# Four pairs of gate tiles as seven block products, and buffers of their own in all pairs of that form

## The chip, the cores and the metric

The kernel runs on one core of a Trainium2 chip. Such a core has TensorE (matrix products into eight accumulator banks), VectorE, ScalarE, GpSimd and SyncE, which work side by side, each through its own queue of instructions in order; transfers from memory run beside them on DMA queues that SyncE and GpSimd fill. In the profile the engines are PE (and PEld for its weight loads), DVE (VectorE), ACT (ScalarE), POOL (GpSimd) and SP (SyncE). The metric is the device time of one execution in microseconds.

## The reference

One decoder layer on x of 512 tokens by 1024 features, all in float32:

```python
proj = h @ w_in[l]
q, k, v, p, g = jnp.split(proj, [...], axis=-1)      # 512, 512, 512, 512 and 2 x 1024 columns
y_attn = moba_attention(q, k, v, rel_bias) @ w_branch_attn[l]
y_pool = multiscale_pool(p, w_pool_group[l], pool_scale[l]) @ w_branch_pool[l]
gates = sigmoid(g).reshape(B, S, 2, D)
mixed = gates[:, :, 0] * y_attn + gates[:, :, 1] * y_pool
h = layer_norm(ALPHA * h + mixed @ w_out[l], ln1_g[l], ln1_b[l])
a, u = jnp.split(h @ w_ffn_in[l], 2, axis=-1)        # 2 x 2816 columns
a = causal_dwconv(a, conv_w[l], conv_b[l])           # three taps along the tokens
f = (gelu(a) * u) @ w_ffn_out[l]
h = layer_norm(ALPHA * h + f, ln2_g[l], ln2_b[l])
```

The change concerns two products: the gate columns of `h @ w_in`, and `h @ w_ffn_in`.

## The kernel before

**Exact products from short ones.** TensorE multiplies operands of a shorter format (fp32r). So each float32 operand is split in two: ScalarE copies it to the short format (the high part, L69), VectorE subtracts that copy from the source (the low part, L70). A product is then three: high by high, high by low, low by high (`mm3`, L182 to 186). In the profile, rows of L184, L185 and L186 are these three.

**Weights.** All weights come in pieces of 128 by 1024, 512 KB, listed in `chunks` in the order of their use. `weights(i)` sees to it that the list has been fetched to LEAD = 3 pieces ahead; `fetch` takes the next: a load by SyncE into one of three raw buffers (`wraw`, L116), and the split into rings of five (`whi`, `wlo`). `state["limit"]` holds the fetching back where buffers further on do not exist yet.

**The stages.** x arrives transposed, is split, and stays as xT_hi and xT_lo. An input tile (`in_tile`) is 128 columns of w_in: 24 matmuls of 512 columns into a bank. `order` is the sequence of such tiles: q, k, p (pool) and 16 gate tiles, where the gate of feature block f has two tiles, f (attention branch) and 8 + f (pool branch). Attention works on four pairs of heads; `bg()` puts one input tile between its steps (scores, transposes of the weights P, product with V), so that TensorE has work while softmax runs. Behind the last product with V, which ends near 163 us, the remaining nine gate tiles run. The first twelve gate tiles are copied to `gates` by VectorE and their sigmoid is taken later; the last four (NLATE) go through ScalarE's sigmoid straight into `late`. zT (pool output) and oT (attention output) are split right behind attention. Then follow the branch products (br, with VectorE multiplying by the gates and GpSimd merging), the output projection (wo), layer norm, the feed-forward input, its output, and the last layer norm.

**Seven products in place of eight.** A feature block f of the feed-forward input is a pair: a and u, each 128 columns. With the tokens cut in halves (t1, t2) and the inner dimension cut in halves (k1, k2), the pair is a block product of 2 by 2, which can be formed with seven products of blocks in place of eight, when sums and differences of blocks are at hand. The pairs f = 4 to 17 (SEVEN) run in that form; the others are plain (48 matmuls of 512 columns). A pair in the form has four weight pieces:

- A, the chunk of a, loaded;
- X, a sum over halves of u and a: SyncE loads u's right half twice and GpSimd starts a second transfer that adds a's halves into it (`fetch_sums`, L129 to 133), into two buffers `xraw`; the two are issued AHEAD = 5 pieces early;
- D, the right half of u, loaded;
- Y, two sums by VectorE from X and A (L144), into a raw buffer.

Each is then split as any weight. The sums of the activations, T3, T4 and the negatives of T1 and T2 (`t_form`, L663 to 672), are formed and split once. `seven` (L688 to 718) issues 84 matmuls of 256 columns into three banks (sa, sb, sc in the profile), with ScalarE and VectorE adding partial results between them. The last product of a pair, `close`, waits in `pending` until the next pair has issued its second product.

**The order on each engine.** The program is not issued in the order of the Python text: a scheduler plays the program against a timeline of its own and puts each engine's instructions in the order in which they become ready there. Marks in the code can pin an instruction to the program's order or set one behind another. The order so built is fixed; on the chip, each queue works it off and waits where it must.

Of the kernel before, what the change touches and what calls it, by code (L numbers as in the profile page):

```python
# [14 lines left out]
P = 128  # L15
S = 512
# [29 lines left out]
def layer_kernel(ctx: ExitStack, tc: tile.TileContext, xT, x, w_v, w_c, rel_bias, invcnt, w_group,  # L46
# [18 lines left out]
    def split(hi, lo, src, copy=None):  # L65
        if copy:
            copy(hi, src)
        else:
            nc.scalar.activation(hi, src, AF.Copy)  # L69
        nc.vector.tensor_tensor(lo, src, hi.bitcast(F32), op=ALU.subtract)  # L70
# [6 lines left out]
    order += spare  # L77
# [4 lines left out]
    chunks += [w_c[first[n] + j] for n, j in order]  # L82
# [5 lines left out]
    fi_at = {}  # L88
    for f in range(NF):
        for q in "AXDY" if f in SEVEN else "au":  # L90
            fi_at[f, q] = len(chunks)
            chunks.append((f, q) if f in SEVEN else w_fi[2 * f + "au".index(q)])
# [30 lines left out]
    sums = list(SEVEN)  # L123
    xu = None

    def fetch_sums(f):
        x_ = raws[f, "X"] = xu.tile([P, D], F32, tag="xraw", name=f"xraw{f}", bufs=2)
        a, u = w_fi[2 * f], w_fi[2 * f + 1]
# [6 lines left out]
    def fetch_seven(i, f, q):  # L135
        n = S if q == "D" else D
        if q == "X":
            raw = raws[f, "X"]
        else:
            raw = raws[f, q] = wp.tile([P, D], F32, tag="wraw", name=f"wraw{i}", bufs=3)[:, :n]  # L140
        if q == "Y":
            a, x_ = raws[f, "A"], raws[f, "X"]
            for c, o in ((slice(0, S), x_[:, S:]), (slice(S, D), raw[:, :S])):
                nc.vector.tensor_tensor(raw[:, c], o, a[:, c], op=ALU.add)  # L144
        elif q != "X":
            nc.sync.dma_start(raw, w_fi[2 * f] if q == "A" else w_fi[2 * f + 1][:, S:])
# [3 lines left out]
        return hi, lo  # L150

# [30 lines left out]
    def mm3(out_, w, a, start, stop, **kw):  # L182
        (wh, wl), (ah, al) = w, a
        nc.tensor.matmul(out_, wh, ah, start=start, stop=False, **kw)  # L184
# [156 lines left out]
    def in_tile(n):  # L341
        kind, j = order[n]
        wh, wl = split3(weights(C0 + n), KT)
        b = bank(f"{kind}{j}")
        for kt in range(KT):
            mm3(b, (wh[:, kt, :], wl[:, kt, :]), (xT_hi[:, kt, :], xT_lo[:, kt, :]), kt == 0, kt == KT - 1)
# [6 lines left out]
        elif len(gslot) < NKEEP:  # L353
            gslot[j] = gates[:, len(gslot), :]
            nc.vector.tensor_copy(gslot[j], b)
# [55 lines left out]
    def pv(p):  # L411
# [7 lines left out]
        nc.scalar.activation(oT[:, p, :], b, AF.Copy)  # L419
# [5 lines left out]
    def bg(n=1):  # L425
        for _ in range(n):
            if len(todo) > NLATE:
# [6 lines left out]

    bg(3)
    for p in range(pairs):
# [7 lines left out]
        bg()  # L444
        pv(p)
    bg(len(todo))
# [486 lines left out]
```

## Time and profile before

| | |
|---|---|
| time, median of 3 runs | 650.57 us (650.09 to 651.02) |
| the profiled execution | 649.74 us, span 648.0 us |
| granted TensorE clock, mean | 0.996 |
| busy: PE, PEld, DVE, ACT, POOL | 98%, 85%, 69%, 51%, 17% |
| memory traffic over the span | 145 GB/s |

By stage, with TensorE's and VectorE's busy time:

| stretch (us) | what runs | PE busy | DVE busy |
|---|---|---|---|
| 0 to 163 | v, q, k, pool, seven gate tiles, attention | 160.9 | 95.5 |
| 163 to 212 | nine gate tiles; zT and oT split | 49.0 | 18.1 |
| 212 to 256 | branch products and merge | 44.0 | 28.5 |
| 256 to 347 | output projection, layer norm, plain feed-forward pairs | 91.0 | 66.6 |
| 347 to 488 | feed-forward pairs as seven products | 139.0 | 116.9 |
| 488 to 648 | last plain pairs, feed-forward output, layer norm | 151.8 | 123.9 |

The profile gives for each engine the time in which it was busy, and for each idle stretch the event that ended it. An idle time counts only where TensorE, or whatever ends last, stands still for it. In a list of waits, a row "PE sa L184 <- ACT whi L69: 1.9, 2, 1.1" reads: matmuls of line 184 into a bank of that name waited for ScalarE's copies of line 69, 1.9 us in all, twice, 1.1 us the longest. In a timeline, a row is the start in us, the duration, engine, line, operation, output and inputs with their shapes; in square brackets the idle time before it and what ended it. In a list of tiles, three numbers with strokes are the least, the median and the largest duration in ns. In a list of transfers, the last number is the median in us from issue to landing.

### The profile page before, as it was taken

How to read it: one execution, taken by the hardware profiler on the slowest of the kernel's cores; microseconds unless marked ns; L12 is line 12 of the kernel's file. 1: busy time of each engine (PE TensorE's matmuls, PEld its weight loads, DVE VectorE, ACT ScalarE, POOL GpSimd, SP SyncE). 2: the span in 40 equal slices, each digit the busy share in tenths (PEclk: the TensorE clock that was granted, in tenths of full speed). 3: DMA queues.
4: the chain of work that ended last, by engine and by line, in shares of the span. 5: the costliest groups of instructions: out<-in, count | busy, mean ns of one | idle time of the engine just before them, and what ended most of it. 6: DMA issues, size and time to landing. Idle time of an engine off the chain costs nothing.

```text
span 648.0 us, 9322 instructions
## 1 busy us (share of the span) xinstructions
PE 635.7 (98%) x3586; PEld 551.4 (85%) x3586; DVE 449.5 (69%) x666; ACT 328.0 (51%) x475; POOL 111.6 (17%) x153
## 2 busy tenths in 40 slices
PE   9999999999999999999999999999999999999994
PEld 6888787877888888888999999998998888888884
DVE  6466665564532576299667888787986859698596
ACT  6547556675522333215444556455665337465452
POOL 1605361211000123300010101010100201123302
PEclk9999999999999999999999999999999999999998
DMA  9643222212222227404056686677635895989905
GB/s 323 197 166 99 82 81 82 74 67 89 74 95 98 91 98 286 136 1 162 2 150 173 170 208 155 179 179 188 165 128 163 274 264 137 218 188 193 282 4 129
DMA packets 32540, 94.79 MB, mean 146 GB/s; under 512 B 3688, under 2 KB 3944, under 8 KB 32240
## 3 DMA queue, kind: packets, MB, share of 16 engines
q1 hardware_dynamic: 22832, 66.91, 30.4%
q0 software_dynamic: 9088, 26.24, 20.7%
q10 hardware_dynamic: 576, 1.05, 0.5%
q8 instruction: 28, 0.46, 0.3%
q14 instruction: 16, 0.13, 0.1%
HBM read 91.02 MB, written 3.17 MB: 145 GB/s over the span
## 4 chain that ended last, share of the span: by engine, by line
PE 91%; DVE 3%; POOL 2%; DMA 1%; ACT 1%; issue 1%; DVEq 0%; ACTq 0%; POOLq 0%
PE fi L186 5%; PE fi L184 5%; PE fi L185 5%; PE g L184 5%; PE g L186 4%; PE g L185 4%; PE sa L184 4%; PE sa L186 4%; PE sa L185 4%; PE v L285 3%; PE wo L186 2%; PE br L186 2%; PE br L184 2%; PE wo L184 2%; PE wo L185 2%; PE br L185 2%
## 5 line engine op out<-in xcount | busy, mean ns | idle before, releaser
L70 DVE TENSOR_TENSOR wlo<-wraw,whi 128x1024 fp32r<-128x1024 f32 (+1 forms) x119 | 144.1, 1214 | 59.2 <-ACT whi L69 57.7
L69 ACT ACTIVATE whi<-wraw 128x1024 fp32r<-128x1024 f32 (+1 forms) x118 | 117.2, 996 | 131.9 <-PE g L185 23.6
L186 PE MATMUL fi<-hT_hi,wlo 128*128 128x512 f32 (+1 forms) x168 | 56.7, 339 | 0.0
L185 PE MATMUL fi<-hT_lo,whi 128*128 128x512 f32 (+1 forms) x168 | 56.7, 339 | 0.0
L184 PE MATMUL fi<-hT_hi,whi 128*128 128x512 f32 (+1 forms) x168 | 56.4, 340 | 0.0
L184 PE MATMUL g<-xT_hi,whi 128*128 128x512 f32 x128 | 50.3, 393 | 0.0
L186 PE MATMUL g<-xT_hi,wlo 128*128 128x512 f32 x128 | 49.9, 390 | 0.0
L185 PE MATMUL g<-xT_lo,whi 128*128 128x512 f32 x128 | 49.8, 389 | 0.0
L132 POOL DMA_DIRECT2D xraw<-in_w_fi x14 | 17.0, 1215 | 183.7 <-DVE y L624 70.2
L69 ACT ACTIVATE whi<-tw 128x1024 fp32r<-128x1024 f32 (+1 forms) x30 | 29.4, 982 | 21.6 <-DMA tw<-in_w_fo 8.1
L70 DVE TENSOR_TENSOR wlo<-tw,whi 128x1024 fp32r<-128x1024 f32 (+1 forms) x30 | 33.3, 1127 | 8.4 <-ACT whi L69 8.4
L185 PEld LDWEIGHTS fi<-hT_lo,whi 128*128 128x128 f32 x168 | 31.9, 190 | 3.5
L186 PEld LDWEIGHTS fi<-hT_hi,wlo 128*128 128x128 f32 x168 | 31.9, 190 | 3.3
L184 PEld LDWEIGHTS fi<-hT_hi,whi 128*128 128x128 f32 x168 | 31.6, 190 | 3.3
L184 PE MATMUL sa<-hT_hi,whi 128*128 128x256 f32 x112 | 31.9, 285 | 2.0 <-ACT whi L69 1.9
L186 PE MATMUL sa<-hT_hi,wlo 128*128 128x256 f32 x112 | 31.7, 284 | 0.0
L185 PE MATMUL sa<-hT_lo,whi 128*128 128x256 f32 x112 | 31.6, 283 | 0.0
L184 PE MATMUL sb<-T_hi,whi 128*128 128x256 f32 x112 | 31.5, 282 | 0.0
L184 PE MATMUL sa<-nT_hi,whi 128*128 128x256 f32 x112 | 31.5, 281 | 0.0
L186 PE MATMUL sa<-nT_hi,wlo 128*128 128x256 f32 x112 | 31.3, 279 | 0.0
L185 PE MATMUL sa<-nT_lo,whi 128*128 128x256 f32 x112 | 31.3, 279 | 0.0
L185 PE MATMUL sb<-T_lo,whi 128*128 128x256 f32 x112 | 31.3, 279 | 0.0
(250 smaller groups left out, 1762.8 us busy)
## 6 DMA issues: line engine op xcount, KB each, us to landing
wraw<-in_w_fi SPq DMA_DIRECT2D x30, 512.0 KB, 3.6
wraw<-in_w_c SPq DMA_DIRECT2D x28, 512.0 KB, 3.4
tw<-in_w_fo POOLq DMA_DIRECT2D x20, 512.0 KB, 8.3
xraw<-in_w_fi SPq DMA_DIRECT2D x14, 512.0 KB, 4.9
xraw<-in_w_fi POOLq DMA_DIRECT2D x14, 512.0 KB, 5.7
wraw<-in_w_fo SPq DMA_DIRECT2D x10, 512.0 KB, 5.1
tw<-in_w_fo SPq DMA_DIRECT2D x10, 512.0 KB, 6.6
wraw<-in_w_br SPq DMA_DIRECT2D x8, 512.0 KB, 3.3
```

What stands on the lines that cost most here:

```text
L69: nc.scalar.activation(hi, src, AF.Copy)
L70: nc.vector.tensor_tensor(lo, src, hi.bitcast(F32), op=ALU.subtract)
L132: nc.gpsimd.dma_start(v, bass.AP(tensor=a.tensor, offset=a.offset, ap=[[pst, pn], [u.offset + S - a.offset, 2], [est, S]]), accum_op=ALU.add)
L184: nc.tensor.matmul(out_, wh, ah, start=start, stop=False, **kw)
L185: nc.tensor.matmul(out_, wh, al, start=False, stop=False, **kw)
L186: nc.tensor.matmul(out_, wl, ah, start=False, stop=stop, **kw)
L285: nc.tensor.matmul(bs[j], xs_[j][a], (wh, wl)[b], start=kt == 0 and n == 0, stop=False)
```

## The change

The gate pairs of features 4 to 7 (eight tiles, g4 to g7 and g12 to g15) run in the form of seven products, with x in place of the layer-normed activations. `order` now ends with g2, g10, g3, the four pairs ("s", 4) to ("s", 7), and g11. For this:

- The sums of x are formed behind attention: a pool `gx` takes attention's space, SyncE reloads xT in four quarters, `t_form` forms and splits the four sums; attention's last copy to oT is set behind the split of T3, and all later gate work with it. The X of pair 4 is fetched there too; `state["limit"]` holds back pair 4's weights while attention runs. One gate tile fewer runs ahead of the last product with V.
- `fetch_seven`, `s_mm`, `seven`, `t_form`, `pending` serve both stages; a pair is named by its stage and number.
- In both stages D has raw buffers of its own (two for the gates, one for the feed-forward), so that the three `wraw` hold A, Y and plain pieces; the first partial result has a tile p1 of its own in place of a part of y.
- The first matmul of D, and the first of a plain tile that stands while a `close` is pending, are pinned to the program's order. The split of nT1 comes last of the four.
- The zT and oT splits come behind the gates. A gate pair's sum goes through ScalarE's sigmoid as it is, u with a scale of -1, so no copy by VectorE and no later sigmoid is needed for the eight tiles; `late` is allocated earlier, on the other side of memory.

```diff
     spare = [("p", 2), ("p", 3)] + [("g", 8 * g + f) for f in range(KT) for g in range(2)]
     for p in range(1, pairs):
         order += [("q", p), ("k", p), spare.pop(0), spare.pop(0)]
-    order += spare
+    order += [("g", 2), ("g", 10), ("g", 3)] + [("s", f) for f in range(4, KT)] + [("g", 11)]
...
     chunks = [w_v[c] for c in range(4)]
     C0 = len(chunks)
-    chunks += [w_c[first[n] + j] for n, j in order]
+    at = {}
+    pair_of = {}
+    for n, j in order:
+        at[n, j] = len(chunks)
+        if n == "s":
+            pair_of["g", j] = w_c[first["g"] + j], w_c[first["g"] + KT + j]
+            for q in "AXDY":
+                at["g", j, q] = len(chunks)
+                chunks.append((("g", j), q))
+        else:
+            chunks.append(w_c[first[n] + j])
...
     def fetch(pool=None, early=None):
         i = state["next"]
         state["next"] = i + 1
-        while sums and xu and fi_at[sums[0], "X"] <= i + AHEAD:
+        while sums and sums[0][0] in xpool and at[(*sums[0], "X")] <= i + AHEAD:
             fetch_sums(sums.pop(0))
...
+    def fetch_sums(key):
+        x_ = raws[key, "X"] = xpool[key[0]](key[1])
+        a, u = pair_of[key]
...
-    def fetch_seven(i, f, q):
+    def fetch_seven(i, key, q):
         n = S if q == "D" else D
         if q == "X":
-            raw = raws[f, "X"]
-        else:
-            raw = raws[f, q] = wp.tile([P, D], F32, tag="wraw", name=f"wraw{i}", bufs=3)[:, :n]
+            raw = raws[key, "X"]
+        elif q == "D":
+            raw = dpool[key[0]](key[1])
+        else:
+            raw = raws[key, q] = wp.tile([P, D], F32, tag="wraw", name=f"wraw{i}", bufs=3)
         if q == "Y":
-            a, x_ = raws[f, "A"], raws[f, "X"]
+            a, x_ = raws[key, "A"], raws[key, "X"]
             for c, o in ((slice(0, S), x_[:, S:]), (slice(S, D), raw[:, :S])):
                 nc.vector.tensor_tensor(raw[:, c], o, a[:, c], op=ALU.add)
         elif q != "X":
-            nc.sync.dma_start(raw, w_fi[2 * f] if q == "A" else w_fi[2 * f + 1][:, S:])
+            a, u = pair_of[key]
+            nc.sync.dma_start(raw, a if q == "A" else u[:, S:])
         hi = wp.tile([P, D], F32R, tag="whi", name=f"whi{i}", bufs=RING)[:, :n]
         lo = wp.tile([P, D], F32R, tag="wlo", name=f"wlo{i}", bufs=RING)[:, :n]
         split(hi, lo, raw)
         return hi, lo
...
+    def t_form(n, tt, b11, b12, b21, b22):
+        if n in ("nT1", "T3"):
+            v, a = {"nT1": (b11, b11), "T3": (b12, b22)}[n]
+            nc.vector.tensor_tensor(v, a, b12, op=ALU.subtract)
+        else:
+            v, a = {"nT2": (b22, b11), "T4": (b21, b22)}[n]
+            nc.vector.scalar_tensor_tensor(v, a, -1.0, v, op0=ALU.mult, op1=ALU.subtract)
+        if n != "nT1":
+            split_of[n] = split(*tt[n], v)
+        if n == "T4":
+            split(*tt["nT1"], b11)
+
+    def s_mm(key, q, part, act_, b, start):
+        wh, wl = split3(weights(at[(*key, q)]), 4 if q == "D" else KT)
+        for k in range(4):
+            mm3(b, (wh[:, 4 * part + k, :], wl[:, 4 * part + k, :]), (act_[0][:, k, :], act_[1][:, k, :]),
+                start and k == 0, k == 3, q == "D" and k == 0, skip_group_check=not start)
+
+    def seven(key, whole, tt, y, u, done):
+        ba, bb, bc = (bank(f"s{q}{key[0]}{key[1]}") for q in "abc")
+        chain, low, c11 = ba[:, 256:], bb[:, :256], bc[:, :256]
+
+        def b_(k, t):
+            return whole[0][:, k, t], whole[1][:, k, t]
+
+        s_mm(key, "A", 0, b_(k1, t1), chain, True)
+        nc.scalar.activation(y, chain, AF.Copy)
+        s_mm(key, "X", 0, tt["T3"], low, True)
+        nc.scalar.activation(u[:, t2], low, AF.Copy)
+        flush()
+        s_mm(key, "Y", 0, tt["nT2"], chain, False)
+        nc.scalar.activation(u[:, t1], chain, AF.Copy)
+        s_mm(key, "A", 1, b_(k2, t1), c11, True)
+        s_mm(key, "D", 0, tt["T4"], low, False)
+        nc.vector.tensor_tensor(u[:, t1], u[:, t1], low, op=ALU.add)
+        s_mm(key, "X", 1, tt["nT1"], chain, False)
+        nc.vector.tensor_tensor(u[:, t2], u[:, t2], chain, op=ALU.add)
+        nc.vector.tensor_tensor(ba[:, t1], y, c11, op=ALU.add)
+
+        def close():
+            s_mm(key, "Y", 1, b_(k2, t2), chain, False)
+            done(ba, u)
+
+        pending.append(close)
...
-    def mm3(out_, w, a, start, stop, **kw):
+    def mm3(out_, w, a, start, stop, pin=False, **kw):
         (wh, wl), (ah, al) = w, a
-        nc.tensor.matmul(out_, wh, ah, start=start, stop=False, **kw)
+        ins = nc.tensor.matmul(out_, wh, ah, start=start, stop=False, **kw)
+        if pin:
...
     def in_tile(n):
         kind, j = order[n]
-        wh, wl = split3(weights(C0 + n), KT)
+        if kind == "s":
+            seven(("g", j), (xT_hi, xT_lo), tg, p1s[j % 2], gus[j % 2],
+                  lambda ba, u, j=j: gates_done(j, ba, u))
+            return
...
         elif len(gslot) < NKEEP:
-            gslot[j] = gates[:, len(gslot), :]
-            nc.vector.tensor_copy(gslot[j], b)
-        else:
-            gslot[j] = late[:, len(gslot) - NKEEP, :]
-            nc.scalar.activation(gslot[j], b, AF.Sigmoid)
+            nc.vector.tensor_copy(new_gate(j), b)
+            plain.append(j)
+        else:
+            nc.scalar.activation(new_gate(j), b, AF.Sigmoid)
...
+    def gates_done(j, ba, u):
+        nc.scalar.activation(new_gate(j), ba, AF.Sigmoid)
+        nc.scalar.activation(new_gate(KT + j), u, AF.Sigmoid, scale=-1.0)
...
-        nc.scalar.activation(oT[:, p, :], b, AF.Copy)
+        return lambda: nc.scalar.activation(oT[:, p, :], b, AF.Copy)
...
-            if len(todo) > NLATE:
+            if order[todo[0]][0] != "s":
...
+    state["limit"] = at["g", 4, "A"]
...
-        bg()
-        pv(p)
-    bg(len(todo))
+        if p < pairs - 1:
+            bg()
+        o_done = pv(p)
+        if p < pairs - 1:
+            o_done()
     attn.close()
+    late = actp.enter_context(tc.tile_pool(name="late", bufs=1, side="right", reuse_waits="tile")).tile(
+        [P, NLATE, S], F32, name="late")
+    gxs = ExitStack()
+    gx = gxs.enter_context(tc.tile_pool(name="gx", bufs=1, reuse_waits="tile"))
+    gx.tile([P, 16], F32, name="gx_gap")
+    tg = {n: tuple(gx.tile([P, 4, 256], F32R, name=f"g{n}_{q}") for q in ("hi", "lo"))
+          for n in ("nT1", "T3", "nT2", "T4")}
+    gus = [gx.tile([P, S], F32, name=f"gu{c}") for c in range(2)]
+    p1s = [gx.tile([P, 256], F32, name=f"p1_{c}") for c in range(2)]
+    gd = [gx.tile([P, S], F32, name=f"drawg{c}") for c in range(2)]
+    gr = [gx.tile([P, D], F32, name=f"xrawg{c}") for c in range(2)]
+    dpool["g"] = lambda f: gd[f % 2]
+    xpool["g"] = lambda f: gr[f % 2]
+    state["limit"] = WO0 - 1
+    quads = []
+    for k in (k1, k2):
+        for t in (t1, t2):
+            v = gx.tile([P, 4, 256], F32, name=f"quad{len(quads)}")
+            nc.sync.dma_start(v, xT[k.start * P:k.stop * P, t].rearrange("(k p) t -> p k t", p=P))
+            quads.append(v)
+    fetch_sums(sums.pop(0))
+    for n in ("nT1", "T3", "nT2", "T4"):
+        t_form(n, tg, *quads)
+    with ExitStack() as behind:
+        for ins in split_of["T3"]:
+            behind.enter_context(tc.issue_after(ins.ins))
+        o_done()
+        while todo:
+            in_tile(todo.pop(0))
+        flush()
+    gxs.close()
 
...
-    late = bp.tile([P, NLATE, S], F32, name="late")
...
-    while todo:
-        in_tile(todo.pop(0))
...
-            if gslot[8 * g + f].tensor is gates.tensor:
+            if 8 * g + f in plain:
...
     for n in ("nT1", "T3", "nT2", "T4"):
-        t_form(n)
+        t_form(n, tt, *(hraw[:, k, t] for k in (k1, k2) for t in (t1, t2)))
...
     hr.close()
     xus = ExitStack()
     xu = xus.enter_context(tc.tile_pool(name="xu", bufs=1, reuse_waits="tile"))
+    dpool["f"] = lambda f: xu.tile([P, S], F32, tag="draw", name=f"draw{f}", bufs=1)
+    xpool["f"] = lambda f: xu.tile([P, D], F32, tag="xraw", name=f"xraw{f}", bufs=2)
     last = max(SEVEN)
     for f in range(RING // 2, last + 1):
         if f in SEVEN:
-            seven(f)
+            seven(("f", f), (hT_hi, hT_lo), tt, xu.tile([P, 256], F32, tag="p1", name=f"p1f{f}", bufs=2),
+                  xu.tile([P, S], F32, tag="u", name=f"u{f}", bufs=2),
+                  lambda ba, u, f=f: gated(f, ba, u, -1.0))
```

More of the change, by code (lines that the diff above doesn't have):

```diff
@@ L122, in layer_kernel @@
     raws = {}
[L123 to L128, printed above, removed]
+    sums = list(pair_of)
+    xpool = {}
+    dpool = {}
+    def fetch_sums(key):
+        x_ = raws[key, "X"] = xpool[key[0]](key[1])
+        a, u = pair_of[key]
         v = x_.rearrange("p (a c) -> p a c", a=2)
```

78 lines of the change are left out of this document (26 added, 52 removed).

## The prediction

> **What bounds the kernel now.** I read the cores' clock first (0.996 granted, so nothing is throttled), then the page, then the stretches of the two stages that the change touches, then the waits of TensorE and VectorE, and last the timelines around the weights' sums.
>
> ```profile
> span 648.0 us, 9322 instructions
> PE 635.7 (98%) x3586; PEld 551.4 (85%) x3586; DVE 449.5 (69%) x666; ACT 328.0 (51%) x475; POOL 111.6 (17%) x153
> PE 91%; DVE 3%; POOL 2%; DMA 1%; ACT 1%; issue 1%; DVEq 0%; ACTq 0%; POOLq 0%
> ```
> ```profile
> 163.00:212.00 49.00, 49.00 (x221) 40.46 (x218) 18.07 (x22) 17.44 (x25) 0.00 (x0) 1.00 0.29 97
> 330.00:400.00 70.00, 70.00 (x525) 67.17 (x524) 53.77 (x74) 36.32 (x53) 8.56 (x7) 1.00 0.71 180
> 400.00:485.00 85.00, 82.96 (x691) 82.14 (x690) 71.25 (x101) 49.49 (x75) 8.43 (x7) 1.00 0.61 160
> ```
> ```profile
> PE sa L184 <- ACT whi L69: 1.9, 2, 1.1
> ```
>
> TensorE is busy for 98% of the span and carries 91% of the chain that ended last. In the stretches the columns are length, then PE, PEld, DVE, ACT and POOL busy with counts, clock, DMA share, GB/s. From 163 to 212 us, where the gate tiles run that become products, TensorE never stops and VectorE works 18 of 49 us. From 330 to 485 us, where the feed-forward pairs already run as seven products, VectorE is busy 77% and then 84%, the DMA engines 71% and 61%, and TensorE waits only 1.9 us for ScalarE's copies of weights. So the gates are bound by TensorE alone, and the seven-product form brings a stage close to a second bound: VectorE, and the transfers that it waits for.
>
> **The change, part by part.**
>
> ```profile
> 174.40 0.69 DVE L355 COPY gates<-g 128x512 f32<-128x512 f32 x1 [3.23 <-PE g L186]
> 190.72 0.69 DVE L355 COPY gates<-g 128x512 f32<-128x512 f32 x1 [3.35 <-PE g L186]
> ```
> ```profile
> 425.20 0.28 PE L184 MATMUL sc<-hT_hi,whi 128*128 128x256 f32 x1
> 428.06 0.28 PE L184 MATMUL sb<-T_hi,whi 128*128 128x256 f32 x1
> ```
>
> *TensorE's own work.* Each gate copy closes one plain tile; between the two rows lie three tiles, so a tile takes 16.32 / 3 = 5.44 us and a pair 10.88. Between the two feed-forward rows lie 24 matmuls of 256 columns in 2.86 us, 0.119 each; seven products are 84 of them, 10.0 us. The gain is 0.88 a pair, **3.5 us** for four. [...]
>
> *What is late next: the first pair's operands.* The four differences of x need reloaded quarters, four subtractions and four splits.
>
> ```profile
> 316.08 2.56 DVE L667 TENSOR_TENSOR hraw<-hraw 128x1024 f32<-128x1024 f32 x2
> 318.56 1.22 DVE L70 TENSOR_TENSOR nT_lo<-hraw,nT_hi 128x1024 fp32r<-128x1024 f32 x1
> 160.76 1.06 ACT L69 ACTIVATE whi<-wraw 128x1024 fp32r<-128x1024 f32 x1 [4.50 <-PE g L185]
> 161.73 0.62 ACT L471 ACTIVATE gates<-gates 128x512 f32<-128x512 f32 x1
> 157.04 0.42 DVE L408 COPY PT<-tr 128x256 f32<-128x256 f32 x1
> ```
> ```profile
> 141.95 0.40 PE L376 MATMUL sc<-kl,q 128*128 128x512 f32 x1
> ```
> ```profile
> L701 ACT ACTIVATE u<-sb x14: 375/382/386, 351.8 to 485.0; 128x256 f32<-128x256 f32 x14
> L144 DVE TENSOR_TENSOR wraw<-xraw,wraw x14: 683/692/694, 340.5 to 474.1; 128x512 f32<-128x512 f32 x14
> ```
>
> The quarters (2 MB) wait only for the last score matmul, which ends at 142.4 us, and VectorE reaches the first difference behind the last copies of P, near 157 us here; 15 us are ample beside the 3.4 us of one 512 KB weight load (row below), so I cost them at nothing. Without that cover each would cost up to its 3.4 us. The engines' orders in the built program then set the rest. I count from the moment TensorE issues pair 4's first A matmul, right behind g3. It issues 12 (1.4 us). ScalarE then does, in this order, the p1 copy (0.38), the high part of the second difference (1.06), g3's sigmoid (0.62) and the high part of X (1.06): with A's own latency of 0.28 and 0.1 of overlap at each step, X is there 3.1 us after A's last issue. VectorE in turn does g3's copy, the fourth difference, waits for that second high part (to 3.0), then splits and sums in line: 1.22 (4.2), 0.69 (4.8), X's low part 1.22 (6.0), 0.69, 0.69, 1.22 (8.3), a sum for pair 5 (8.9), Y's low part (10.1). TensorE wants Y's low part after 40 matmuls, 4.8 us. Together these are **5.3 us** of idle TensorE (X's 3.1 is part of it).
>
> *What is late after that: the sums of weights.* X is made by two transfers, a load by SP and an accumulating one by POOL, into two buffers; a buffer comes free when its X has been split.
>
> ```profile
> wraw<-in_w_c SPq DMA_DIRECT2D x28, 512.0 KB, 3.4
> xraw<-in_w_fi SPq DMA_DIRECT2D x14, 512.0 KB, 4.9
> xraw<-in_w_fi POOLq DMA_DIRECT2D x14, 512.0 KB, 5.7
> ```
>
> In the gates VectorE frees pair 4's X at 6.0, so pair 6's X lands at 6.0 + 4.9 + 5.7 = 16.6. VectorE reaches the sum that needs it at 13.5 and stands there for 3.1 us; behind it in the queue are the adds that close pair 4 (done near 19.2). TensorE needs those adds before its last product into the same bank, 108 matmuls after the start: 12.9 + 5.3 = 18.2. That is 1.0 us of idle, and by the same pattern about as much in the next two pairs: **3.2 us**. The gate stage so comes out at -3.5 + 5.3 + 3.2 = **+5.0 us**, bounded by -3.5 (all hidden, as TensorE is in 330 to 400) and by +8 (each of the four pairs pays the 3.1 us in full).
>
> *All feed-forward pairs: the D half gets its own buffer.* The three raw buffers now hold only A and Y, so A's load can go one step earlier, and p1 no longer shares y. Nothing in the instruction count changes; what changes is VectorE's order. Before, a pair's Y sum stands directly ahead of the split of the same pair's X:
>
> ```profile
> 417.54 1.23 DVE L70 TENSOR_TENSOR wlo<-xraw,whi 128x1024 fp32r<-128x1024 f32 x1 [0.24 <-ACT whi L69]
> 423.53 0.68 DVE L144 TENSOR_TENSOR wraw<-xraw,wraw 128x512 f32<-128x512 f32 x1
> 424.73 1.22 DVE L70 TENSOR_TENSOR wlo<-xraw,whi 128x1024 fp32r<-128x1024 f32 x1
> ```
> ```profile
> DVE wraw L144 <- DMA xraw<-in_w_fi: 4.9, 1, 4.9
> ```
>
> and the queue stood on an X transfer just once, for 4.9 us. In the built program afterwards the order is, for pairs 12, 13, 14 and 15 (and for 7):
>
> ```
> DVE wraw (Y of 13) <- xraw of 13, A of 13
> DVE wlo  (X of 12) <- xraw of 12
> ```
>
> The next pair's sum stands ahead of this pair's split. But the next X can be loaded only into the buffer that the previous split freed, so there is a loop: split of X(n-1), load 4.9, accumulate 5.7, sum 0.69, split of X(n) 1.22, 12.5 us a turn. TensorE needs 10.0 for a pair. Each such place costs 2.5 us; the four in a row **10 us**, and the one at 7 and the places where the next sum stands directly behind the split (it may wait there too, since one pair's 10.0 is less than the 10.6 of two transfers) I put at 2 more, between nothing and 5. The waits of 1.9 us seen before may go (a gain of at most that), which I leave inside this. **+12 us**, from -1.9 to +17.
>
> [...]
>
> *The rest.* The zT and oT splits, which ran right behind attention, move behind pair 7's second X product, which frees their space.
>
> ```profile
> 163.80 2.18 ACT L69 ACTIVATE zT_hi<-zT 128x512 fp32r<-128x512 f32 x4
> 164.52 2.50 DVE L70 TENSOR_TENSOR zT_lo<-zT,zT_hi 128x512 fp32r<-128x512 f32 x4 [1.44 <-ACT zT_hi L69]
> ```
>
> Four take 2.18 us on ScalarE and 2.50 on VectorE, behind one weight split (1.06 + 1.22), so 4.8 us; g11 (5.4) and the last product (1.4) cover them before the first branch tile wants zT: nothing, and up to 4.8 without that cover. Pair 4's D load waits for the end of P times V on SP's queue, with pair 5's A load behind it; both land within two loads of 3.4 us, ahead of the 8.9 at which VectorE wants the A: nothing, at most the 3.4 of one. POOL's first accumulate stands behind the scaling of P and is due 5.7 us later, before VectorE asks near 162: nothing. Five gate copies of 0.69 go from VectorE; they would save time only where VectorE is late, and the walk above is by the order without them. The pinned matmuls fix an order and issue nothing.
>
> **Sum.** The profiled execution took 649.74 us (span 648.0), 0.83 below the median of 650.57. 649.74 + 5.0 + 12 = 666.7, or 667.6 against the median; I say **667**.
>
> **The rivals.**
> 1. *The two transfers keep up* (they land in the 3.6 us of the plain feed-forward load: 3.6 + 3.6 + 1.9 = 9.1, under 10.0). For it: A's load leaves one step earlier and collides less. Against: the accumulates landed at 5.7 in the median. Then only the gate stage loses: 649.74 + 5.0 - 1.9 = 653; cases between it and mine fill the rest up to 657.
>
> ```profile
> wraw<-in_w_fi SPq DMA_DIRECT2D x30, 512.0 KB, 3.6
> ```
>
> 2. *Faster*: VectorE stays ahead of TensorE in both stages, as from 330 to 400 us, where TensorE was busy 70.00 of 70.00. The place is VectorE's queue; it decides if the X chain falls from 10.6 to 8.1 us or less and the 5.3 us at pair 4 is covered. Price -3.5 - 1.9: 644.3. Against: the first copies stand in ScalarE's order behind a product just issued, whatever the DMAs do.
> 3. *The loop binds in all pairs*: ten more places lose 1 us or more: 677 or beyond. Against: there the sum stands behind the split.
>
> **Chances.** Mine 0.58 (657 to 675), rival 1 0.18 (651.9 to 657), rival 2 0.12, between rivals 2 and 1 so that nothing is to be told (within 0.2%, 1.3 us, about what a measurement of this kernel can tell) 0.04, rival 3 0.08. The range 649 to 675 takes in the first, the second and the fourth, and leaves out 0.20. Faster 0.12, same 0.04, slower 0.84.
>
> **What would show it.** In the gate stage a TensorE idle of about 3 us on ScalarE's copy of X, in a stage 5 us longer; VectorE waiting for X transfers there and in the feed-forward pairs 3 to 5 us at a time, five times or more; sevens at 11 us or more a pair in the second half. No waits on X transfers and pairs at 10.0 us would prove the loop wrong; an idle TensorE under 2 us at pair 4 the first part.

## The result, and the profile after

The changed kernel takes 682.58 us (median; 679.84 to 684.21) against 650.77 (650.09 to 651.02): a ratio of 1.0486, with a 95% interval of 1.0449 to 1.0524. It is 31.8 us slower; 16 were forecast, and 682.58 lies above the range. The profiled execution took 684.21 us, the slowest of four.

The page of the changed kernel (total, busy times, the chain that ended last), and its two stages in the list of stretches, whose columns are as in the prediction:

```profile
span 682.5 us, 9690 instructions
PE 646.4 (95%) x3730; PEld 565.5 (83%) x3730; DVE 469.4 (69%) x697; ACT 342.4 (50%) x499; POOL 115.5 (17%) x157
PE 74%; DMA 11%; DVE 8%; issue 3%; ACT 2%; POOL 2%; DVEq 0%; POOLq 0%; ACTq 0%
```
```profile
163.00:222.00 59.00, 52.36 (x374) 49.76 (x373) 40.47 (x53) 34.19 (x53) 2.39 (x2) 0.94 0.51 143
357.00:584.00 227.00, 207.89 (x1437) 194.59 (x1436) 156.95 (x208) 111.87 (x158) 20.74 (x20) 0.97 0.61 160
```

The same two stretches before:

```profile
163.00:213.00 50.00, 50.00 (x226) 41.27 (x223) 18.07 (x22) 18.14 (x26) 0.00 (x0) 1.00 0.28 95
348.00:549.00 201.00, 198.96 (x1434) 188.07 (x1433) 161.69 (x211) 111.38 (x157) 21.12 (x20) 1.00 0.68 182
```

The first branch matmul starts at 221.5 us in place of 212.3, 9.2 later. From the first feed-forward product in the new form to the first matmul of the feed-forward output it is 226.7 us (357.2 to 583.9) in place of 201.4 (348.0 to 549.4), 25.3 more. That is the whole loss. TensorE is idle for 6.6 and 19.1 us in these stretches, where it was idle for none and 2.0. But idle time is not all: the granted clock, 1.00 in both before, is 0.94 and 0.97. The matmuls show where. In TensorE's timeline, the stop at pair 4, and what follows it:

```profile
169.72 0.39 PE L253 MATMUL sbg<-gT_hi,whi 128*128 128x256 f32 x1 [2.88 <-ACT whi L69]
...
170.82 0.41 PE L256 MATMUL scg<-xT_lo,whi 128*128 128x256 f32 x1
171.03 0.41 PE L257 MATMUL scg<-xT_hi,wlo 128*128 128x256 f32 x1
...
176.41 0.28 PE L256 MATMUL sag<-gnT_lo,whi 128*128 128x256 f32 x1
176.52 0.28 PE L257 MATMUL sag<-gnT_hi,wlo 128*128 128x256 f32 x1
...
186.22 0.39 PE L253 MATMUL sag<-xT_hi,whi 128*128 128x256 f32 x1 [2.54 <-DVE sag L213]
```

After the stop of 2.88 us the granted clock is 0.50 from 170.17 us on, and matmuls start 0.21 us apart, for 3.4 us; later they start 0.12 apart again. Summing the starts that lie too far apart behind each long stop gives 1.5 to 2.4 us each; there are five such stops in this execution, two in the gates and three in the feed-forward, 8.9 us together. All stops over 0.3 us in both stages come to 25.4 (1.9 before). With the slow matmuls that is 32.4 us more than before, against 34.5 that the span grew; what is left, and the little that the seven products gave back, lies in shorter delays that I did not follow one by one.

In the feed-forward, VectorE's timeline shows the sums of weights standing on X transfers. First a pair from the middle, then three of the places where the next pair's sum stands ahead of this pair's split; last the row of VectorE's waits:

```profile
390.67 0.69 DVE L158 TENSOR_TENSOR wraw<-xraw,wraw 128x512 f32<-128x512 f32 x1 [4.07 <-DMA xraw<-in_w_fi]
391.28 0.74 DVE L741 SCALAR_TENSOR_TENSOR y<-saf,cvp,y 128x511 f32<-128x511 f32 x1
391.94 0.41 DVE L210 TENSOR_TENSOR u<-u,sbf 128x256 f32<-128x256 f32 x1
...
394.58 0.43 DVE L213 TENSOR_TENSOR saf<-p1f,scf 128x256 f32<-128x256 f32 x1
...
436.80 0.69 DVE L158 TENSOR_TENSOR wraw<-xraw,wraw 128x512 f32<-128x512 f32 x1 [4.92 <-DMA xraw<-in_w_fi]
...
438.13 1.22 DVE L70 TENSOR_TENSOR wlo<-xraw,whi 128x1024 fp32r<-128x1024 f32 x1
...
450.43 0.69 DVE L158 TENSOR_TENSOR wraw<-xraw,wraw 128x512 f32<-128x512 f32 x1 [5.30 <-DMA xraw<-in_w_fi]
451.04 1.22 DVE L70 TENSOR_TENSOR wlo<-xraw,whi 128x1024 fp32r<-128x1024 f32 x1
...
463.39 0.69 DVE L158 TENSOR_TENSOR wraw<-xraw,wraw 128x512 f32<-128x512 f32 x1 [4.75 <-DMA xraw<-in_w_fi]
```
```profile
DVE wraw L158 <- DMA xraw<-in_w_fi: 35.6, 8, 5.3
```

The loop of the prediction is there: from 436.80 to 450.43 to 463.39 a turn takes 13.6 and 13.0 us (12.5 was worked out). But VectorE waits on X in eight places, not five: at the first pair, as in the kernel before; at five sums that stand ahead of a split (a sixth such sum, at 363.18, stands behind 1.8 us of idle for which the profile shows no cause); and at two, 390.67 and 490.84, that stand directly behind one. At 390.67 the adds are queued behind the sum (L210, L213), and the next splits of weights behind them. Three more sums, at 401.88, 413.59 and 424.80, wait 1.6 to 3.0 us for A's load, which the prediction did not count. TensorE's own waits in these pairs show what comes late by this, mostly the low parts of weights, which VectorE makes, and then the adds:

```profile
PE saf L257 <- DVE wlo L70: 6.8, 5, 2.3
PE sbf L257 <- DVE wlo L70: 4.4, 5, 1.4
PE saf L253 <- DVE saf L213: 4.4, 3, 2.5
```

### The profile page after: what moved, and what is told of

Same layout as the page of the kernel before. It is cut to its first block, busy times and chain, and to the rows that moved or that the text cites. A ratio compares the mean times of both kernels' runs of the same rounds, so it can differ in the third digit from the quotient of the medians.

```text
span 682.5 us, 9690 instructions
## 1 busy us (share of the span) xinstructions
PE 646.4 (95%) x3730; PEld 565.5 (83%) x3730; DVE 469.4 (69%) x697; ACT 342.4 (50%) x499; POOL 115.5 (17%) x157
## 4 chain that ended last, share of the span: by engine, by line
PE 74%; DMA 11%; DVE 8%; issue 3%; ACT 2%; POOL 2%; DVEq 0%; POOLq 0%; ACTq 0%
DMA xraw<-in_w_fi 9%; PE fi L253 4%; PE fi L257 4%; PE fi L256 4%; PE v L356 3%; DVE wlo L70 3%; PE g L253 2%; PE g L257 2%; PE br L253 2%; PE g L256 2%; PE wo L257 2%; PE br L257 2%; PE wo L253 2%; PE wo L256 2%; PE br L256 2%
## 5 line engine op out<-in xcount | busy, mean ns | idle before, releaser
L69 ACT ACTIVATE whi<-wraw 128x1024 fp32r<-128x1024 f32 (+1 forms) x104 | 108.0, 1044 | 99.2 <-PE saf L256 16.9
L257 PE MATMUL saf<-nT_hi,wlo 128*128 128x256 f32 x112 | 32.5, 290 | 6.6 <-DVE wlo L70 6.6
L257 PE MATMUL sbf<-T_hi,wlo 128*128 128x256 f32 x112 | 32.9, 294 | 4.4 <-DVE wlo L70 4.4
L253 PE MATMUL saf<-hT_hi,whi 128*128 128x256 f32 x112 | 32.7, 292 | 4.6 <-DVE saf L213 4.4
L253 PE MATMUL saf<-nT_hi,whi 128*128 128x256 f32 x112 | 32.5, 290 | 3.3 <-ACT whi L69 3.3
L743 ACT ACTIVATE y<-y 128x512 f32<-128x512 f32 x22 | 13.9, 630 | 42.7 <-DVE y L742 42.7
L253 PE MATMUL sbf<-T_hi,whi 128*128 128x256 f32 x112 | 32.5, 290 | 0.0
L256 PE MATMUL sbf<-T_lo,whi 128*128 128x256 f32 x112 | 32.3, 289 | 0.0
L256 PE MATMUL saf<-hT_lo,whi 128*128 128x256 f32 x112 | 32.3, 288 | 0.0
L256 PE MATMUL saf<-nT_lo,whi 128*128 128x256 f32 x112 | 32.2, 287 | 0.0
L257 PE MATMUL saf<-hT_hi,wlo 128*128 128x256 f32 x112 | 31.9, 288 | 0.2 <-DVE wlo L70 0.2
```

Source lines behind the costliest of these rows:

```text
L69: first_ = nc.scalar.activation(hi, src, AF.Copy)
L253: ins = nc.tensor.matmul(out_, wh, ah, start=start, stop=False, **kw)
L256: nc.tensor.matmul(out_, wh, al, start=False, stop=False, **kw)
L257: nc.tensor.matmul(out_, wl, ah, start=False, stop=stop, **kw)
L743: nc.scalar.activation(y, y, AF.Gelu)
```

## The experiments

Each time stands against runs of the kernel before on the same chip (medians 650.5 to 650.9). The theories: (1) two separate losses, the gates and the place of the Y sums in VectorE's queue; (2) the transfers themselves became slower; and (3) one of the parts alone, or their meeting, is to blame.

**The gates alone.** The changed kernel, with the feed-forward as before (the lines for its pin and its order of the splits are left out here):

```diff
-        elif q == "D":
+        elif q == "D" and key[0] == "g":
...
-            seven(("f", f), (hT_hi, hT_lo), tt, xu.tile([P, 256], F32, tag="p1", name=f"p1f{f}", bufs=2),
+            seven(("f", f), (hT_hi, hT_lo), tt, ytiles[f % 2][:, t1],
```

> The four gate pairs as seven products as in the changed kernel; the feed-forward pairs as before (D in the ring of three raw buffers, first partial result in y, nothing pinned there, old order of the splits). Theory 1 (two separate losses: the branch stage starts 9.2 us later in the changed kernel, and 25.3 us are lost in the feed-forward pairs because VectorE's queue has the next pair's Y sum ahead of this pair's X split): 650.8 + 9 = 660, between 657 and 663, and in the feed-forward no wait of VectorE on an X transfer beyond the one of 5 us that the kernel before has. Rival 2 (the added transfers and products of the gate stage disturb the later stages too, by displaced loads or a lowered clock): 668 or more. Rival 3 (the gate form itself is free and only the buffers cost): 651 or less.

Measured: 659.76 us, 1.0136 (1.0115 to 1.0157). The gate part costs 9.0 us by itself, and VectorE waits on an X transfer once (4.8 us) in the feed-forward.

**The feed-forward part alone**, on the kernel before (the lines for the pin and the order of the splits are left out here):

```diff
+        elif q == "D":
+            raw = xu.tile([P, S], F32, tag="draw", name=f"draw{f}", bufs=1)
...
-        y = ytiles[f % 2]
+        y = xu.tile([P, 256], F32, tag="p1", name=f"p1f{f}", bufs=2)
```

> Only the feed-forward part on the kernel before: D in a buffer of its own, p1 of its own, D's first matmul pinned, nT1's split last; gates plain. Theory 1: the built order has six pairs whose Y sum stands ahead of the split of the X before, as in the changed kernel, so 650.8 + 25 = 676, between 671 and 680, with TensorE's granted clock under 1 behind each idle of about 2.5 us or more. Rival 2 (the loss in the feed-forward comes from the gate stage): 651 to 656.

Measured: 672.10 us, 1.0324 (1.0296 to 1.0352), 21.3 us. With the 9.0 of the gates that is 30.3 of the 31.8: two separate losses.

**D's buffer without p1.**

```diff
-        y = xu.tile([P, 256], F32, tag="p1", name=f"p1f{f}", bufs=2)
+        y = ytiles[f % 2][:, t1]
```

> As the run before, but p1 lies in y again: only D's own buffer, the pin and the split order are left. The built order has three such places (6 ahead of 5, 7 ahead of 6, 12 ahead of 11) in place of six. Theory 1 (each place costs): about half of the 25 us, so 663, between 658 and 668. Rival 2 (the buffer and the earlier loads as such cost, by contention of transfers): as with p1, 673 to 680. Rival 3 (p1 alone is the cause): 651.

Measured: 666.10 us, 1.0238 (1.0202 to 1.0273). D's buffer, with the pin and the split order, brings 15 of the 21 us, though no instruction is added. What the buffer changes is when A's load can go, and with it the built order; that the pin and the split order have no share in this was not shown.

**The order of the pairs kept.** The changed kernel, with each Y sum set behind the split of the X before it:

```diff
+                if (key[0], key[1] - 1) in xsplit:
+                    behind.enter_context(tc.issue_after(xsplit[key[0], key[1] - 1].ins))
```

> The changed kernel with one more order edge: each pair's Y sum stands behind the split of the X of the pair before it on VectorE. Same buffers, transfers, products. Theory 1: the loop split, load, accumulate, sum, split is gone, the feed-forward loss of 25 us with it, and what is left is the gates' 9: 660, between 656 and 664. Rival 2 (slower transfers: the accumulating ones land in 7.0 us in place of 5.7): 672 or more, and VectorE still waits on X transfers.

Measured: 672.47 us, 1.0330 (1.0293 to 1.0367). The swap of the pairs accounts for 10.1 us and no more; theory 1 as it stood missed by 12. VectorE's timeline shows what is left:

```profile
393.16 1.22 DVE L70 TENSOR_TENSOR wlo<-xraw,whi 128x1024 fp32r<-128x1024 f32 x1 [0.26 <-ACT whi L69]
398.01 0.69 DVE L161 TENSOR_TENSOR wraw<-xraw,wraw 128x512 f32<-128x512 f32 x1 [3.62 <-DMA xraw<-in_w_fi]
398.62 0.74 DVE L747 SCALAR_TENSOR_TENSOR y<-saf,cvp,y 128x511 f32<-128x511 f32 x1
399.28 0.41 DVE L216 TENSOR_TENSOR u<-u,sbf 128x256 f32<-128x256 f32 x1
```

The sum now stands directly behind the split, and so ahead of the gating (L747), the adds (L216, L219) and the next splits of weights. TensorE waits for the last two:

```profile
PE saf L263 <- DVE wlo L70: 8.8, 6, 2.7
PE saf L259 <- DVE saf L219: 3.6, 3, 1.8
```

In the kernel before the sum stood behind the add that completes the pair two before (L711): in the lines of the prediction it starts 4.8 us after the end of that split (417.54 plus 1.23, to 423.53), with adds, gating and three splits of weights between.

**The sum behind that add.**

```diff
+                if key[0] == "f" and ("f", key[1] - 2) in added:
+                    behind.enter_context(tc.issue_after(added["f", key[1] - 2].ins))
...
+        added[key] = nc.vector.tensor_tensor(ba[:, t1], y, c11, op=ALU.add)
```

> The changed kernel with one edge on VectorE: a feed-forward pair's Y sum stands behind the add that completes the pair two before it (sa from p1 and sc), which is where it stands in the kernel before, 4 us later in the queue than in the changed kernel and in the run with the order kept. Buffers, transfers and products stay. Theory 1, mended (the place of the sum in VectorE's queue is the whole feed-forward loss, by the swapped pairs and by standing ahead of the adds): 660, between 657 and 663, the value of the gates alone. Rival 2 (D's own buffer and the earlier loads slow the transfers, accumulate 7.0 us in place of 5.7, and this costs wherever the sum stands): 665 to 672.

Measured: 655.53 us, 1.0073 (1.0058 to 1.0088): 27 us less than the changed kernel by one edge, and below the gates alone. The transfers are about as slow as before the mend (the median of the accumulating ones is 6.6 us; 7.0 in the changed kernel, 5.7 in the kernel before), and of VectorE's 14 first sums only one still waits for them:

```profile
399.12 0.43 DVE L217 TENSOR_TENSOR saf<-p1f,scf 128x256 f32<-128x256 f32 x1
399.45 0.68 DVE L161 TENSOR_TENSOR wraw<-xraw,wraw 128x512 f32<-128x512 f32 x1
```
```profile
DVE wraw L161 <- DMA xraw<-in_w_fi: 5.3, 1, 5.3
```

So theory 2 falls: slower transfers are still there, and the loss is gone. (p1 alone and the pin alone were not tried.)

**That edge on the feed-forward part alone** (the kernel of the second experiment):

```diff
+                if f - 2 in added:
+                    behind.enter_context(tc.issue_after(added[f - 2].ins))
...
+        added[f] = nc.vector.tensor_tensor(ba[:, t1], y, c11, op=ALU.add)
```

> The kernel before with the feed-forward part of the change alone (D's buffer, p1, pin) and the edge that puts each Y sum behind the add of the pair two before. Theory 1 (own buffers cost nothing once the sum stands late in the queue, and the waits of 1.9 us on ScalarE's copies go): 650.8 - 2.9 = 648, between 647 and 650; 2.9 is what branch start to feed-forward output is shorter in the run with that edge than in the kernel before (334.2 against 337.1). Rival (the gain seen there came with the gates): 650 to 652.

Measured: 647.16 us, 0.9948 (0.9931 to 0.9965). This is faster than both kernels: gates as before, D and p1 with tiles of their own, and the edge. Its stretch has no idle TensorE and a full clock:

```profile
347.00:488.00 141.00, 141.00 (x1176) 140.44 (x1175) 114.91 (x162) 84.19 (x124) 14.20 (x12) 1.00 0.66 169
```

**A third X buffer in the gates** (on the gates alone).

```diff
-    gr = [gx.tile([P, D], F32, name=f"xrawg{c}") for c in range(2)]
+    gr = [gx.tile([P, D], F32, name=f"xrawg{c}") for c in range(3)]
...
-    xpool["g"] = lambda f: gr[f % 2]
+    xpool["g"] = lambda f: gr[f % 3]
```

> The gates alone (feed-forward as before) with a third buffer for X in the gate stage, so that pair 6's X needn't wait for pair 4's split. Theory 1 (TensorE's stop of 2.5 us at 186 us is VectorE standing on pair 6's X, with the adds of pair 4 behind it, and 1.6 us of slow clock follow): 659.8 - 4.2 = 655.6, between 654 and 657.5. Rival (the next late thing takes its place, A's load or ScalarE's copies): 658 to 660.

Measured: 663.08 us, 1.0189 (1.0174 to 1.0204), slower than the 659.76 without it. The stop at 186 us is gone, but there is a new one of 11.7 us, and VectorE shows why:

```profile
166.42 1.23 DVE L179 TENSOR_TENSOR quad<-quad,quad 128x1024 f32<-128x1024 f32 x1 [6.56 <-DMA quad<-in_xT]
```
```profile
177.91 0.58 PE L253 MATMUL sbg<-gT_hi,whi 128*128 128x256 f32 x1 [11.74 <-ACT whi L69]
```

A quarter of x arrived late. With the same buffer and the order of pair 4 written out (`after` sets what follows behind both splits of what it names, `upto` fetches pair 4's pieces so far):

```diff
+    t_form("T3", tg, *quads)
+    with after("T3"):
         o_done()
+        upto("X")
+    with after((G4, "X")):
+        t_form("nT2", tg, *quads)
+    with after("nT2"):
+        upto("Y")
+    with after((G4, "Y")):
+        t_form("T4", tg, *quads)
+        with after("T4"):
+            split_of["nT1"] = split(*tg["nT1"], quads[0])
...
```

> As the run with the third buffer, and the order on ScalarE and VectorE at pair 4 written out: split of T3, split of X, T2 and its split, D and Y of pair 4, T4 and its split, nT1's split, then pair 5's weights. Theory 1 (the stop of 2.9 us at 169 us and its 1.8 us of slow clock come from X's split standing behind the first partial result's copy, T2's split and a sigmoid): another 4.5 us, 651, and with the smaller stops of the gate stage gone too 648: between 646 and 652. Rival (VectorE's line of splits and sums is itself too long for pair 4): 653 to 656.

Measured: 671.08 us, 1.0315 (1.0292 to 1.0338), with a stop of 12.4 us at the same place. Next the buffer was moved behind the quarters in memory (with the old order):

```diff
-    gr = [gx.tile([P, D], F32, name=f"xrawg{c}") for c in range(3)]
+    gr = [gx.tile([P, D], F32, name=f"xrawg{c}") for c in range(2)]
...
-    xpool["g"] = lambda f: gr[f % 3]
+    xpool["g"] = lambda f: gr[(f - 4) % 3]
...
             quads.append(v)
+    gr.append(gx.tile([P, D], F32, name="xrawg2"))
```

> As the run with the third X buffer, but the buffer lies behind the four quarters of xT in memory, so that the quarters keep the space they had; it serves pair 6. Theory 1 (the 11.7 us at 178 us in that run were the quarters, pushed by 4 KB into space that attention's last product held until 163 us; the third buffer itself takes away the stop at 186 us): 659.8 - 4.2 = 655.6, between 654 and 657.5. Rival (the buffer's own load waits for attention's end, with the loads of D and A behind it in SyncE's queue): 658 to 664.

Measured: 656.43 us, 1.0084 (1.0059 to 1.0109). The late quarters were a matter of place: with the buffer behind them they are in time again, so the 4 KB ahead of them had pushed them into space that attention held to its end. And the third buffer does take the stop at 186 us away. With the written order of above on top:

> As the run before, with the order of pair 4 written out: T3, X, T2, D and Y, T4, nT1, then pair 5's weights. Theory 1 (2.9 us of stop and 1.8 us of slow clock at 169 us come from X's split standing behind other work): 655.6 - 4.7 = 651, between 648 and 653. Rival (VectorE's line of splits and sums is itself too long for pair 4): 654 to 658.

Measured: 656.98 us, 1.0097 (1.0062 to 1.0133), no gain; the time lies where the rival put it, though not for the rival's reason alone, as a later run shows. All mends together (this one, and the feed-forward with its edge):

> All together: the changed kernel with the Y sums behind the add of the pair two before, the third X buffer of the gates behind the quarters, and the written order at pair 4. Theory 1 (the parts add up): 655.5 - 4.2 - 4.7 = 647, between 644 and 650, faster than both kernels. Rival (VectorE's line in the gates keeps TensorE waiting): 650 to 655.

Measured: 654.33 us, 1.0054 (1.0039 to 1.0069), 7 us above what the parts would add up to. ScalarE, in the run with the written order, shows one fault of mine:

```profile
163.38 0.60 ACT L510 ACTIVATE oT<-ob 128x512 f32<-128x512 f32 x1 [3.10 <-PE ob L508]
163.88 1.05 ACT L69 ACTIVATE whi<-xrawg 128x1024 fp32r<-128x1024 f32 x1
```

Attention's last copy waits 3.1 us for TensorE, and X's split stands behind it; its transfer had landed by then, for in the run that follows the same split starts at 160.33 us. With the copy behind X, and T2's difference ahead of T3's low part (two moves, not tried apart):

```diff
-        o_done()
...
-    with after((G4, "X")):
-        t_form("nT2", tg, *quads)
+    t_form("nT2", tg, *quads, edge=lambda: after((G4, "X")))
     with after("nT2"):
+        o_done()
```

> As the run with all mended, but X's high part stands ahead of attention's last copy to oT on ScalarE, and the difference T2 ahead of T3's low part on VectorE: in the run with the written order ScalarE waited 3.1 us for attention's last product with X's split behind that copy, and TensorE's stop at 173 us was 3.5 us. Theory 1 (with X split by 163 us VectorE's line ends some 3 us earlier, the stop falls under 1.5 us, no slow clock follows): 654.3 - 2.5 - 5 = 647, between 644 and 649. Rival (VectorE's splits and sums for pair 4 stay the bound): 651 to 654.

Measured: 649.78 us, 0.9975 (0.9960 to 0.9990). The long stop is gone; three short ones are left (the first, of 0.48 us, at 170.58), and a slow clock all the same. The last row below, of TensorE alone, ends with the granted clock, the DMA share and GB/s:

```profile
172.86 0.39 PE L265 MATMUL sbg<-gT_hi,whi 128*128 128x256 f32 x1 [0.83 <-ACT gT_hi L69]
174.12 0.58 PE L268 MATMUL sbg<-gT_lo,whi 128*128 128x256 f32 x1 [0.87 <-DVE gT_lo L70]
```
```profile
173.00:178.00 5.00, 4.13 (x19) 0.53 1.04 208
```

So even mended, the gates in the new form are 2.6 us slower than the plain ones beside the same feed-forward (649.78 against 647.16). Whether a better order still would make them pay is open.

**One stop by itself.** In the kernel before, a gate tile's first matmul waits for one copy, or a chain of four, on ScalarE (the diff is that of four; both runs also pin the first matmul of each of these later gate tiles to the program's order):

```diff
+        if (kind, j) == ("g", 14):
+            src = state["bank"]
+            for c in range(4):
+                dst = b if c == 4 - 1 else pause[c % 2]
+                nc.scalar.activation(dst, src, AF.Copy)
+                src = dst
```

> The kernel before with one stop of TensorE put in, ahead of the gate tile of index 14: its first matmul waits for one copy on ScalarE that reads the bank of the tile before and stands behind that tile's sigmoid, about 1.4 us. Both theories (a stop costs its length; a stop costs its length and, over some limit, slow matmuls behind it): 650.6 + 1.4 = 652.0.

> As the run before with a chain of four copies, a stop of about 3.1 us. Theory clock (behind a stop over some limit between 2.2 and 2.3 us, matmuls run at about half speed for 3.5 us): the stop plus 1.6, so 655.3, and the granted clock is under 1 in the 5 us behind the stop. Rival (a stop costs its length): 653.7.

Measured: 653.43 us (1.0036, 1.0022 to 1.0049) and 656.92 us (1.0085, 1.0068 to 1.0102), 2.8 and 6.3 above the kernel before. The stops came out longer than I had set them:

```profile
198.96 0.50 PE L184 MATMUL g<-xT_hi,whi 128*128 128x512 f32 x1 [1.94 <-ACT g L351]
```
```profile
202.72 0.79 PE L184 MATMUL g<-xT_hi,whi 128*128 128x512 f32 x1 [3.90 <-ACT g L351]
```
```profile
200.00:205.00 5.00, 2.27 (x5) 1.82 (x6) 1.00 (x1) 2.58 (x5) 0.00 (x0) 0.64 0.31 105
205.00:210.00 5.00, 5.00 (x17) 3.96 (x16) 0.00 (x0) 0.00 (x0) 0.00 (x0) 0.68 0.00 0
```

Between the two runs the stop grows by 1.96 us and the time by 3.5. The rest fits the slow clock behind the long one: in the profiled execution it is 0.50 from 202 to 208 us, and 17 matmuls of 512 columns run in the 5 us from 205 us, where 24 do in the profile of the short stop, at 1.00. That execution, of 660.96 us, is the slowest of seven; from the first gate tile to the first branch matmul it takes 122.5 us, against 118.0 in the profile of the short stop and 115.8 before. By the intervals the short stop costs 1.4 to 3.2 us, which agrees with its length of 1.94; the long one costs 4.4 to 6.6, which is more than its 3.90.

## Why the prediction was wrong

The direction and both places were right; the size was not: 16 us against 31.8.

*TensorE's own work* (-3.5). The two forms cost what was worked out, 0.119 and 0.227 us a matmul. But only 2.0 us came: of the plain tile that no longer runs ahead of the last product with V, seven matmuls (1.6 us) run behind it, and that product ends no earlier (163.3 us for 163.0). Behind it stand 31 plain and 336 small matmuls, 47.0 us, in place of 216 plain ones, 49.0.

*The first pair's operands* (+5.3). TensorE waited 2.88 us for X, where 3.1 were worked out, and 0.33 for Y's low part. The rest of the wait for Y was there, but TensorE filled it with slow matmuls, 1.9 us of excess. Together 5.1: right in sum by luck, with another content.

*The adds behind the sums* (+3.2). One stop of 2.54 us at pair 6, where three of about 1 were forecast, and one of 0.9 at pair 7, which is not of this kind: it ends with a copy by ScalarE (L207). With 1.6 of slow clock on top it is 5.0 in all. At pair 6 the mechanism was as described: its X landed at 183.4, 18.2 us after the start of pair 4 (16.6 was worked out), and a third buffer took the long stop away. The gate stage thus comes to -2.0 + 5.1 + 5.0 = 8.1 of the 9.0 measured.

*The feed-forward* (+12, up to +17). **Here the prediction failed**, at the step "the places where the next sum stands directly behind the split I put at 2 more, between nothing and 5". The loop was right: with the swaps undone the time falls by 10.1 us, and 10 stood in the sum for it (that they agree so closely is in part luck: the turns were longer, 13.0 and 13.6 us, and six places were swapped, not five). But a sum that stands directly behind the split stands ahead of the gating, the adds and the next splits of weights as well. TensorE waits for those, 3.6 us for the adds and 8.8 for the low parts, and slow clock comes on top. Moving the sum behind the add took another 16.9 us (672.47 to 655.53). Of these, 3.4 (650.53 to 647.16, gates plain) or 4.2 (659.76 to 655.53, gates in the new form) are a gain over the feed-forward of before, so the loss by this place is 12.7 to 13.6 us, where the step had 2. I had read the order only for which of two weights comes first, and had not looked at what else had stood between them.

*The waits of 1.9 us that may go.* They went: no wait of TensorE is left in that stage of the fastest run. The term was right in sign and hidden by the order.

*The rest* (nothing). The branch stage waits for no split of zT; the quarters and pair 4's D cost nothing in the changed kernel. That the quarters' cover depends on where they lie in memory was seen only when 4 KB moved them.

*What no step had* is the clock. I took each idle us at its own length, with the clock at 1.00 in every row of before that the prediction shows; the longest stop in its two stages was 1.1 us. In the changed kernel 8.9 us are slow matmuls, which start 0.21 us apart in place of 0.12, with a granted clock of 0.50. Stops of 2.30, 2.54, 2.55, 2.88 and 3.33 us brought it in this kernel, and one of 1.97 in the feed-forward part alone.

Rival 3 (the loop in all pairs, 677 or beyond) came nearest in time, and its condition is not what happened: the sum stood and waited ahead of a split for four pairs in a row and at pair 7, and the rest was its place in the queue.

## What to carry to other kernels

A buffer more changes no instruction, yet it lets a load go earlier, and a scheduler may then put what uses it earlier into an engine's queue, in front of work that another engine waits for; so read the built order around every instruction that waits on a transfer, on both sides, and write down with an edge what has to stand ahead of it. Where a stage has VectorE busy for 80% of the time, the place of one waiting instruction decided more here (27 us) than all that the buffers themselves could give (3.4 to 4.2). And do not count a stop of the matmul engine at its length alone: here, stops of 2.30 to 2.88 us brought a slow clock of 3.4 us that cost about 1.6 us more, and stops of 3.33 and 3.90 us one of 6.8 us that cost about 2.4.

## What the hardware showed that was not expected

The length of a stop does not by itself decide whether the clock falls. In the executions profiled here the granted clock was 0.50 behind a stop of 1.97 us, and 1.00 behind one of 2.11 us (the rows below). Three short ones, of 0.48, 0.83 and 0.87 us within 4 us, came ahead of a granted clock of 0.53 in the 5 us from 173 us (the rows of the last mended run), while 1.45 and 1.32 us at 439 and 443 us of the changed kernel left it at 1.00.

The profile of the changed kernel shows what its slow stretches have in common. Between 160 and 610 us the granted clock is 0.50 in five of them, for 3.41 us from 170.17, 187.23, 395.45 and 470.54 us and for 6.83 us from 494.43; it is 1.00 elsewhere. The later four begin 5, 66, 88 and 95 times 3.41 us behind the first. In the 3.41 us ahead of each, TensorE was busy for 0.53, 1.01, 0.86, 1.28 and 0.81 us; in the two stretches of 3.41 us from 436.40 us, with the stops of 1.45 and 1.32 us, it was busy for 1.97 and 2.09 us, and the clock stayed at 1.00. The stop of 1.97 us (the feed-forward part alone, to 371.36 us) lies inside one stretch of that length, and in the next the clock is 0.50:

```profile
368.78:372.19 3.41, 1.44 (x13) 1.23 (x12) 2.71 (x4) 1.06 (x1) 0.00 (x0) 1.00 0.01 1
372.19:375.60 3.41, 3.41 (x19) 3.41 (x18) 3.38 (x7) 0.90 (x2) 0.00 (x0) 0.50 0.71 214
```

The stop of 2.11 us (D's buffer without p1, to 370.71 us) is shared by two, 1.27 us of it in the first and 0.84 in the second; TensorE was busy for 2.14 and 2.58 us, and the clock is 1.00 in both:

```profile
366.46:369.87 3.41, 2.14 (x19) 1.94 (x17) 1.04 (x2) 1.06 (x1) 0.00 (x0) 1.00 0.11 18
369.87:373.29 3.42, 2.58 (x21) 2.55 (x21) 3.42 (x6) 0.00 (x0) 0.00 (x0) 1.00 0.36 117
```

The starts of matmuls tell the same. Cut the changed kernel's profile between 160 and 610 us into stretches of 3.41 us that begin with the slow ones, and take those that hold matmuls of 256 columns alone: 3 to 11 started in each of the six that a slow stretch followed (one of the six was slow itself), and 14 to 29 in each of the 62 others. This is read from the profile afterwards; no run shifted a stop by a part of 3.41 us on purpose, so that the place of a stop is the cause was not shown.

And transfers that landed later did not decide the time: the accumulating X transfers took 6.6 us in the run of 655.53 us and 7.1 in that of 672.47, against 5.7 before.
